# A second superblock's down projection as seven-product quads in one pipeline with gate and up

## The chip, the cores and the metric

The kernel runs on one core of a Trainium2 chip. The metric is the device time of one execution in microseconds. Three runs of the kernel before took 1899.77, 1903.79 and 1904.42 us; their median is 1903.79 us.

## The reference

One decoder layer over 2048 tokens of 1024 features, in float32:

```
xn = rmsnorm(x); z = xn @ w_in + b_in            # a, gate, p: 512 columns each
y_conv = silu(layernorm(causal_depthwise_conv31(a * sigmoid(gate))))
y_pool = per group of 128 channels: (trailing mean over 2/4/8/16 - token) @ w_pool, times a scale
h = x + concat(y_conv, y_pool) @ w_out
n = rmsnorm(h)
h = h + (silu(n @ w_gate) * (n @ w_up)) @ w_down  # 1024 -> 2816 -> 1024
out = rmsnorm(h)
```

## The kernel before, in words

The tokens are two superblocks (`a0`, `a1`, class `Sup`) of 1024 tokens, each two halves of 512. Features lie on the partitions, in tiles of 128. Each float32 operand of a product is split in two parts (`split`, L194): ScalarE casts the high part (L195), VectorE subtracts it for the low part (L196). A product is then three matmuls of 128x128 on 512 columns, high by high, high by low and low by high (`mm3`, L202 to L206). So each tile that goes into a product costs one ScalarE and one VectorE instruction.

SBUF is held in two arenas. `arena` has 17 slots for float32 staging, `arena_r` 36 units for split operands. Both give the range that has been free longest, in the order in which the program asks; activations (`R`) take four units, weights (`W`) two or one. PSUM has one `chain` tile of two banks and three tiles of two banks that `ps2` gives in turn.

The stages: input projection (`in_tile`, `in_evac`), convolution and pooling (mostly VectorE, woven in as a background generator), output projection and row norm (`mix_out`, `norm`), gate and up (`gate_up`), down (`down`, `down_last`), and the final norm.

Gate and up already use a seven-product scheme. A `Quad` is two output tiles by eight k-tiles by two halves, seen as a 2x2 by 2x2 block product, and done as seven products of 12 matmuls in place of eight. `put_t` forms the seven combinations of the activations (the factors `t[1]` to `t[7]`), `Quad.sums` and `Quad.put` the combinations of the weights, and `Quad.result` adds or multiplies what leaves PSUM. Bank copies on ScalarE (L911, L916, L918) keep partial sums between products, and the next product into that bank waits for them. In the steady loop of `gate_up` (L707 on) the products of a quad come in the order 1, 2, 6, 5, 7, 4, 3, with product 1 of the next quad ahead of 4 and 3. There are 22 quads, gate and up in turn, and each pair's product is stored in `at_d` (L926).

Down is done in three groups of four, four and three of these stored tiles (`GROUPS`). For each group `down_load` reads and splits the tiles, and `down` then runs eight output tiles, each with 8 k-tiles (6 in the last group) for both halves, adding to `h`, which it reads from and writes back to `h_d`. The weights are made by `Dense`, two ahead (`prime`). In the second superblock `down_last` does the last group together with the final norm.

`turn` joins the output projection and the first two quads: it steps generators by hand, so that the norm of the second half (`rows`: small matmuls for row sums, a power on POOL, a diagonal on VectorE; `spread`: matmuls that broadcast it; then scaling by L634) lies beside the first products. The order of the instructions on an engine follows the program, but the framework moves one ahead when by its own estimate an earlier one isn't ready; all DMAs of this part are issued on SP's queue in order.

Of the kernel before, what the change touches and what calls it, by code (L numbers as in the profile page):

```python
# [33 lines left out]
GROUPS = ((0, 4), (4, 8), (8, 11))  # L34
G32 = HALO + TT + 2
# [68 lines left out]
def block_kernel(ctx: ExitStack, tc: tile.TileContext, x, xt, wi, wo, wop, wg, wu, wd, wp, par, out):  # L104
# [44 lines left out]
    h_d = [dram(f"h_d{s}", NQ, 2 * TT) for s in range(NS)]  # L149
    at_d = [dram(f"at_d{s}", NFP, 2 * TT) for s in range(NS)]  # L150
# [34 lines left out]
    class W(Buf):  # L185


        WHERE = (range(8 * RU, NR), range(7 * RU, NR), range(NR))
# [19 lines left out]
    class Dense:  # L208


        def __init__(self, src, halves=False, parts=None):
# [22 lines left out]
        def mms(self, accs, ks, mov):  # L234

            ks = list(ks)
            for n, k in enumerate(ks):
                ww, c = self(k)
                r = mov[k // 2].v
                for b, acc in accs:  # L240
                    mm3(acc, ww, c, (r[:, 0, k % 2, b], r[:, 1, k % 2, b]), n == 0, n == len(ks) - 1)
# [26 lines left out]
    class Rms:  # L268
# [83 lines left out]
    class Sup:  # L352
# [176 lines left out]
        def ln(self):  # L529
# [21 lines left out]
            var.rows(1.0 / CC, LN_EPS, chain if first else None)  # L551
# [75 lines left out]
        def norm(self, b, hr):  # L627

            hr.rows(1.0 / D, RMS_EPS)
# [21 lines left out]
        def gate_up(self):  # L651
# [6 lines left out]
            at = None  # L658
            quads = []
            for n in range(2 * NFP):  # L660
                quads.append(Quad(self, n))
# [45 lines left out]
            for n in range(2, 2 * NFP):  # L707
# [25 lines left out]

        def down_load(self, g):
            a = []
# [7 lines left out]
            return a  # L743

        def down(self, g, a):
# [4 lines left out]
            ws = Ahead([lambda m=m: Dense(wd[g][m]) for m in range(KD)], 1)  # L750
            ws.prime(2)
# [19 lines left out]
        def down_last(self, g, a):  # L771

            n = len(a)
            ws = []
            ah = Ahead([lambda m=m: Dense(wd[g][m]) for m in range(KD)], 1)
# [55 lines left out]
    class Quad:  # L831
# [6 lines left out]
        at = None  # L838

        def __init__(self, sup, n):  # L840
# [5 lines left out]
            self.ch = chain_bank[n % 2]  # L846

# [27 lines left out]

        def result(self, a, b, acc, extra=None):
# [8 lines left out]

        def product(self, p):
            if p == 1:
                self.acc = ps2("quad")
                if self.gate:
                    Quad.at = B4("at")  # L890
                self.at = Quad.at
                self.o = self.at.v
            b1, b5, ch = self.acc[:, 0], self.acc[:, 1], self.ch
            dst = {1: b1, 2: b1, 5: b5, 3: b5}.get(p, ch)
            r = self.sup.t[p].v
# [9 lines left out]
            if self.n == 2 * NFP - 1:  # L905
                self.sup.t.pop(p).free()
# [15 lines left out]
            elif p == 3:  # L922
                self.result(0, 1, b5, self.s.v[:, 0])
                self.s.free()
                if not self.gate:
                    nc.sync.dma_start(at_d[self.sup.s][self.fp], self.at.ap)  # L926
                    self.at.free()
# [78 lines left out]
    pa1 = a0.in_tile(in0.get(), "pa")  # L1006
    a0.x_spread()
    a0.in_evac(0, pa, pg)
# [55 lines left out]
    def turn(s, gu):  # L1064
# [18 lines left out]
        nm = s.norm(1, s.hr)  # L1083
        step(gu)
        step(nm, 2)
        step(gu)
        step(nm)
# [10 lines left out]
    beside(a0.down(0, a0.down_load(0)), bg, 3, 1)  # L1098
    beside(a0.down(1, a0.down_load(1)), bg, 4, 1)
    run(bg)  # L1100
    dn = a0.down(2, a0.down_load(2))
# [70 lines left out]
```

## Time and profile before

| | |
|---|---|
| median of three runs | 1903.79 us |
| profiled execution | 1902.86 us |
| its span | 1901.1 us |
| TensorE matmul busy | 1841.0 us, 7995 records |
| VectorE busy | 1234.7 us |
| ScalarE busy | 623.2 us |
| HBM read, written | 189.19 MB, 73.49 MB |

The profiled execution is one run; its span goes from the first to the last instruction. A busy TensorE is no measure of its rate: matmuls overlap, so the start-to-start distance of matmuls and the number of records in a stretch say more. PEclk is the clock granted to TensorE, as a share of full speed. Some matmul records are missing.

### The profile page before, as it was taken

How to read it: one execution, taken by the hardware profiler on the slowest of the kernel's cores; microseconds unless marked ns; L12 is line 12 of the kernel's file. 1: busy time of each engine (PE TensorE's matmuls, PEld its weight loads, DVE VectorE, ACT ScalarE, POOL GpSimd, SP SyncE). 2: the span in 40 equal slices, each digit the busy share in tenths (PEclk: the TensorE clock that was granted, in tenths of full speed). 3: DMA queues.
4: the chain of work that ended last, by engine and by line, in shares of the span. 5: the costliest groups of instructions: out<-in, count | busy, mean ns of one | idle time of the engine just before them, and what ended most of it. 6: DMA issues, size and time to landing. Idle time of an engine off the chain costs nothing.

```text
span 1901.1 us, 19811 instructions
## 1 busy us (share of the span) xinstructions
PE 1841.0 (97%) x7995; PEld 1497.5 (79%) x7995; DVE 1234.7 (65%) x1359; ACT 623.2 (33%) x796; POOL 51.4 (3%) x41
## 2 busy tenths in 40 slices
PE   8999999998999999998999999899999999999996
PEld 6777887876788888877788888678888888888885
DVE  4989997488997999992542546866554545523235
ACT  5255124244333333341221323433333333412110
POOL 0103200000000000000000000000000000000000
PEclk9999999999999999998999999899999999999998
DMA  7263125523422232143583753155131113635422
GB/s 284 75 212 123 67 90 172 205 78 122 167 79 88 73 116 78 67 188 133 190 313 130 285 199 111 47 198 199 45 132 67 67 67 147 252 144 215 154 85 89
DMA packets 70235, 263.96 MB, mean 139 GB/s; under 512 B 7168, under 2 KB 11392, under 8 KB 56320
## 3 DMA queue, kind: packets, MB, share of 16 engines
q1 hardware_dynamic: 68848, 260.52, 38.1%
q10 hardware_dynamic: 1296, 2.19, 0.3%
q8 instruction: 62, 1.02, 0.2%
q14 instruction: 29, 0.24, 0.0%
HBM read 189.19 MB, written 73.49 MB: 138 GB/s over the span
## 4 chain that ended last, share of the span: by engine, by line
PE 83%; DVE 8%; DMA 4%; ACT 1%; issue 1%; POOL 0%; POOLq 0%; DVEq 0%; SPq 0%; ACTq 0%
PE pd L206 8%; PE pd L204 8%; PE pd L205 8%; PE quad L204 8%; PE quad L206 8%; PE quad L205 8%; PE chain L204 6%; PE chain L205 6%; PE chain L206 6%; PE px L204 3%; PE px L205 3%; PE px L206 3%; DVE arena_r L196 2%; DVE arena L491 2%; PE pa L206 1%
## 5 line engine op out<-in xcount | busy, mean ns | idle before, releaser
L195 ACT CAST arena_r<-arena 128x1024 fp32r<-128x1024 f32 (+3 forms) x375 | 364.4, 984 | 848.1 <-PE pd L205 228.9
L196 DVE TENSOR_TENSOR arena_r<-arena,arena_r 128x1024 fp32r<-128x1024 f32 (+3 forms) x375 | 422.2, 1138 | 246.5 <-ACT arena_r L195 215.5
L491 DVE SCALAR_TENSOR_TENSOR arena<-arena,par_sb 128x1024 f32<-128x1024 f32 (+1 forms) x240 | 287.2, 1212 | 2.3
L204 PE MATMUL quad<-arena_r 128*128 128x512 f32 x704 | 276.2, 393 | 11.7 <-ACT arena_r L195 10.8
L204 PE MATMUL pd<-arena_r 128*128 128x512 f32 x704 | 276.1, 392 | 9.9 <-ACT arena_r L195 9.1
L205 PE MATMUL quad<-arena_r 128*128 128x512 f32 x704 | 276.2, 392 | 0.8 <-DVE arena_r L196 0.8
L206 PE MATMUL pd<-arena_r 128*128 128x512 f32 x704 | 275.1, 391 | 1.8 <-DVE arena_r L196 1.8
L206 PE MATMUL quad<-arena_r 128*128 128x512 f32 x704 | 275.8, 392 | 0.0
L205 PE MATMUL pd<-arena_r 128*128 128x512 f32 x704 | 274.6, 390 | 0.0
L204 PE MATMUL chain<-arena_r 128*128 128x512 f32 x528 | 212.1, 402 | 4.9 <-ACT arena L916 2.8
L205 PE MATMUL chain<-arena_r 128*128 128x512 f32 x528 | 207.1, 392 | 0.9 <-DVE arena_r L196 0.9
L206 PE MATMUL chain<-arena_r 128*128 128x512 f32 x528 | 207.1, 392 | 0.0
L761 DVE TENSOR_TENSOR arena<-pd,arena 128x1024 f32<-128x1024 f32 x40 | 48.9, 1223 | 187.8 <-PE pd L206 186.7
L204 PEld LDWEIGHTS quad<-arena_r 128*128 128x128 f32 x704 | 133.3, 190 | 41.7 <-ACT arena_r L195 12.1
L204 PEld LDWEIGHTS pd<-arena_r 128*128 128x128 f32 x704 | 132.7, 188 | 39.1 <-ACT arena_r L195 10.2
L206 PEld LDWEIGHTS pd<-arena_r 128*128 128x128 f32 x704 | 132.5, 188 | 31.4 <-DVE arena_r L196 4.0
L205 PEld LDWEIGHTS quad<-arena_r 128*128 128x128 f32 x704 | 133.2, 189 | 29.3 <-DVE arena_r L196 1.9
L206 PEld LDWEIGHTS quad<-arena_r 128*128 128x128 f32 x704 | 133.3, 189 | 28.2 <-DVE arena_r L196 0.4
L205 PEld LDWEIGHTS pd<-arena_r 128*128 128x128 f32 x704 | 132.6, 188 | 27.9 <-issue 0.5
L204 PEld LDWEIGHTS chain<-arena_r 128*128 128x128 f32 x528 | 99.6, 189 | 38.0 <-ACT chain L911 8.8
L205 PEld LDWEIGHTS chain<-arena_r 128*128 128x128 f32 x528 | 99.9, 189 | 21.8 <-DVE arena_r L196 2.2
L206 PEld LDWEIGHTS chain<-arena_r 128*128 128x128 f32 x528 | 99.7, 189 | 21.8
(135 smaller groups left out, 2082.8 us busy)
## 6 DMA issues: line engine op xcount, KB each, us to landing
arena<-h_d SPq DMA_DIRECT2D x28, 1024.0 KB, 5.6
arena<-in_wg SPq DMA_DIRECT2D x44, 512.0 KB, 5.1
arena<-in_wu SPq DMA_DIRECT2D x44, 512.0 KB, 5.1
at_d<-arena SPq DMA_DIRECT2D x22, 1024.0 KB, 4.4
arena<-at_d SPq DMA_DIRECT2D x22, 1024.0 KB, 5.7
h_d<-arena SPq DMA_DIRECT2D x20, 1024.0 KB, 4.3
arena<-in_wd SPq DMA_DIRECT2D x32, 512.0 KB, 4.4
arena<-in_x SPq DMA_DIRECT2D x12, 1024.0 KB, 6.4
```

Of the source, the lines that this page charges most:

```text
L195: nc.scalar.copy(hi, y)
L196: tt(out=lo, in0=y, in1=hi.bitcast(F32), op=ALU.subtract)
L204: nc.tensor.matmul(acc, lhsT=w[:, 0, c], rhs=hi, start=start, stop=False, **kw)
L205: nc.tensor.matmul(acc, lhsT=w[:, 0, c], rhs=lo, start=False, stop=False, **kw)
L206: nc.tensor.matmul(acc, lhsT=w[:, 1, c], rhs=hi, start=False, stop=stop, **kw)
L491: stt(out=v, in0=u.ap[:, j : j + n], scalar=w, in1=v, op0=ALU.mult, op1=ALU.add)
L761: tt(out=v, in0=acc, in1=v, op=ALU.add)
```

## The change

For the second superblock the first two down groups become quads. `Quad.close` forms from each stored pair the seven combinations and writes them to a new scratch tensor `t_d` (four of them in place or untouched from the tile, three from a second tile `tx`, by four subtractions). `factors(g)` reads back and splits the seven factors of a group; it is stepped once per product of the last quad before the group, right where the old factor of that product number is freed (`follow`). `DownQuad` is a `Quad` with two tiles of `w_down` as weights, `h` as the tensor to add to, and the new factors. The eight down quads go into the same list as the 22, so the loop of `gate_up` runs over 30. `down_load` becomes a generator that is stepped in the same way in the last quad of either superblock and ends with the first two weight loads of the next `down`. The k-tiles of the down weights are laid out with the first halves of all tiles of a group ahead of the second halves (`pairs`, `place`).

Besides: the row norm of the second half uses a bank of the first quad, which is taken earlier (`begin`), and its rows stand after the first product in the order, its spread after the second. The spread of the first input norm stands ahead of the second input tile. Weights take units 28 to 35 in turn; before, 32 to 35 came first.

```diff
-        WHERE = (range(8 * RU, NR), range(7 * RU, NR), range(NR))
+        WHERE = (range(7 * RU, NR), range(NR))
...
-        def __init__(self, src, halves=False, parts=None):
+        def __init__(self, src, halves=False, parts=None, pairs=None):
+            self.place = (lambda k: (k % pairs, k // pairs)) if pairs else (lambda k: (k // 2, k % 2))
...
-            pv = ps2("pv") if bank is None else bank
-            f = flat(pv)
+            f = flat(ps2("pv")) if bank is None else bank
...
-            for n in range(2 * NFP):
-                quads.append(Quad(self, n))
+            quads = [Quad(self, n) for n in range(2 * NFP)]
+            if self.s:
+                self.td = [{} for _ in range(STRASSEN)]
+                for g in range(STRASSEN):
+                    quads[-1].follow = self.factors(g)
+                    quads += [DownQuad(self, g, q, len(quads) + q) for q in range(NQ)]
+                g = STRASSEN
+            else:
+                g = 0
+            quads[-1].follow = self.follow = self.down_load(g)
...
-            yield
-            for q in (q0, q1):
-                q.product(1)
-                q.product(2)
+            q0.begin()
+            q1.begin()
+            self.bank = q0.acc[:, 1]
+            yield
+            q0.product(1)
+            yield
+            q0.product(2)
+            yield
+            q1.product(1)
+            q1.product(2)
             q1.mid()
...
-            for n in range(2, 2 * NFP):
+            for n in range(2, len(quads) - 2):
...
+        def factors(self, g):
+            for p, i in ((1, 0), (2, 2), (6, 5), (5, 1), (7, 4), (4, 6), (3, 3)):
+                t = B4("tl")
+                nc.sync.dma_start(t.ap, t_d[g][:, i].rearrange("p n t -> p (n t)"))
+                self.td[g][p] = r = R("td")
+                for j in range(2):
+                    split(r.v[:, 0, j], r.v[:, 1, j], t.v[:, j])
+                t.free()
+                yield
...
         def down_load(self, g):
...
-            return a
+                yield
+            self.ws = Ahead([lambda m=m: Dense(wd[g][m], pairs=GROUPS[g][1] - GROUPS[g][0]) for m in range(KD)], 1)
+            self.ws.prime(2)
+            yield
...
+        def close(self):
+            if self.gate:
+                return
+            g, j = divmod(self.fp, 4)
+            if self.sup.s and g < STRASSEN:
+                o = self.o
+                tx = B4("tx")
+                for dst, i0, i1 in (
+                    (tx.v[:, 0, 0], o[:, 1, 1], o[:, 0, 1]),
+                    (o[:, 0, 1], o[:, 0, 1], o[:, 0, 0]),
+                    (tx.v[:, 0, 1], o[:, 1, 1], o[:, 0, 1]),
+                    (tx.v[:, 1, 0], o[:, 1, 0], tx.v[:, 0, 1]),
+                ):
+                    tt(out=dst, in0=i0, in1=i1, op=ALU.subtract)
+                nc.sync.dma_start(t_d[g][:, :4, j], self.at.ap.rearrange("p (n t) -> p n t", n=4))
+                nc.sync.dma_start(t_d[g][:, 4:, j], tx.ap[:, : 3 * T].rearrange("p (n t) -> p n t", n=3))
+                tx.free()
+            else:
+                nc.sync.dma_start(at_d[self.sup.s][self.fp], self.at.ap)
+            self.at.free()
...
-            if self.n == 2 * NFP - 1:
-                self.sup.t.pop(p).free()
+            if self.follow:
+                self.t.pop(p).free()
+                step(self.follow)
...
+    class DownQuad(Quad):
+        def __init__(self, sup, g, q, n):
+            self.sup, self.q = sup, q
+            self.s1, self.s2 = wd[g][2 * q], wd[g][2 * q + 1]
+            self.w = {}
+            self.ch = chain_bank[n % 2]
+            self.t = sup.td[g]
+            self.follow = None
+        def open(self):
+            self.h = B4("h")
+            nc.sync.dma_start(self.h.ap, h_d[self.sup.s][self.q])
+        def close(self):
+            nc.sync.dma_start(h_d[self.sup.s][self.q], self.h.ap)
+            self.h.free()
+        def result(self, a, b, acc, extra=None):
+            dst = self.h.v[:, a, b]
+            if extra is not None:
+                tt(out=dst, in0=dst, in1=extra, op=ALU.add)
+            tt(out=dst, in0=acc, in1=dst, op=ALU.add)
...
-    pa1 = a0.in_tile(in0.get(), "pa")
+    w = in0.get()
     a0.x_spread()
+    pa1 = a0.in_tile(w, "pa")
...
-        nm = s.norm(1, s.hr)
+        nm = s.norm(1, s.hr, s.bank)
         step(gu)
-        step(nm, 2)
+        step(nm)
         step(gu)
+        step(nm)
+        step(gu, 2)
         step(nm)
...
-    for g in range(len(GROUPS) - 1):
-        run(a1.down(g, a1.down_load(g)))
-    run(a1.down_last(len(GROUPS) - 1, a1.down_load(len(GROUPS) - 1)))
+    run(a1.follow)
+    for g in range(STRASSEN, len(GROUPS) - 1):
+        run(a1.down(g))
+        run(a1.down_load(g + 1))
+    run(a1.down_last(len(GROUPS) - 1))
```

## Rows read from the trace of the kernel before

**Rows 1.** The page, busy time of each engine, its share and instructions.
```profile
PE 1841.0 (97%) x7995; PEld 1497.5 (79%) x7995; DVE 1234.7 (65%) x1359; ACT 623.2 (33%) x796; POOL 51.4 (3%) x41
```

**Rows 2.** Timeline of PE, late gate/up of superblock 1: start, duration, engine, operation.
```profile
1611.77 0.39 PE L204 MATMUL quad<-arena_r 128*128 128x512 f32 x1
...
1612.45 0.39 PE L204 MATMUL quad<-arena_r 128*128 128x512 f32 x1
```

**Rows 3.** Windows: stretch, length, busy us (records) per engine, PEclk, DMA share, GB/s.
```profile
40.00:60.00 20.00, 16.84 (x68) 13.41 (x67) 10.45 (x9) 5.33 (x5) 0.38 (x2) 0.91 0.21 75
...
420.00:460.00 40.00, 31.54 (x122) 22.70 (x121) 33.65 (x38) 17.91 (x22) 1.01 (x1) 0.91 0.33 117
...
460.00:840.00 380.00, 379.11 (x1661) 309.91 (x1660) 350.96 (x382) 135.28 (x182) 0.00 (x0) 1.00 0.28 101
...
840.00:880.00 40.00, 30.56 (x124) 23.99 (x123) 16.30 (x17) 9.25 (x10) 0.00 (x0) 0.87 0.54 193
...
960.00:980.00 20.00, 20.00 (x89) 16.54 (x89) 2.96 (x4) 1.53 (x2) 0.00 (x0) 1.00 0.93 347
...
1200.00:1240.00 40.00, 31.97 (x113) 23.52 (x112) 33.06 (x39) 17.36 (x20) 1.01 (x1) 0.83 0.19 66
...
1240.00:1620.00 380.00, 380.00 (x1671) 310.44 (x1669) 202.16 (x252) 131.97 (x180) 2.48 (x1) 1.00 0.31 114
...
1620.00:1660.00 40.00, 39.51 (x173) 31.92 (x172) 26.33 (x26) 19.39 (x22) 0.00 (x0) 1.00 0.77 289
...
1660.00:1820.00 160.00, 160.00 (x708) 132.48 (x707) 46.18 (x40) 24.93 (x25) 0.00 (x0) 1.00 0.43 157
```

**Rows 4.** Groups by line, 1255 to 1620 us: busy us, mean ns, idle before.
```profile
L196 DVE TENSOR_TENSOR arena_r<-arena,arena_r 128x1024 fp32r<-128x1024 f32 x59 | 72.1, 1221 | 55.0 <-ACT arena_r L195 55.0
...
L195 ACT CAST arena_r<-arena 128x1024 fp32r<-128x1024 f32 x59 | 62.0, 1050 | 77.5 <-PE quad L205 75.2 <-DVE arena L866 2.3
```

**Rows 5.** DMA issues: count, KB each, median us from issue to landing.
```profile
arena<-at_d SPq DMA_DIRECT2D x22, 1024.0 KB, 5.7
```

**Rows 6.** Timeline of ScalarE at the superblock-1 seam, its idle time in brackets.
```profile
1640.52 4.84 ACT L195 CAST arena_r<-arena 128x1024 fp32r<-128x1024 f32 x5 [1.17 <-DMA arena<-at_d]
```

**Rows 7.** Timeline of all engines at the superblock-0 seam.
```profile
845.79 0.32 SPq L738 DMA_DIRECT2D arena<-at_d  x1
...
853.42 0.32 SPq L926 DMA_DIRECT2D at_d<-arena  x1
...
853.79 0.43 SPq L224 DMA_DIRECT2D arena<-in_wd  x1
...
859.57 1.04 ACT L195 CAST arena_r<-arena 128x1024 fp32r<-128x1024 f32 x1 [6.54 <-DMA arena<-in_wd]
...
860.67 0.80 PE L204 MATMUL pd<-arena_r 128*128 128x512 f32 x1 [8.73 <-ACT arena_r L195]
```

**Rows 8.** Timeline of the turn into superblock 1's gate/up.
```profile
1201.86 0.57 ACT L911 COPY chain<-quad 128x512 f32<-128x512 f32 x1 [0.94 <-PE quad L206]
...
1203.63 0.68 DVE L299 TENSOR_TENSOR arena<-arena 128x512 f32<-128x512 f32 x1
...
1207.16 0.95 PE L316 MATMUL pv<-ones,arena 128*128 128x1 f32 x8
...
1210.90 0.71 PE L346 MATMUL rb<-arena_r,ones_r 128*128 128x512 f32 x2
...
1211.78 2.06 DVE L634 SCALAR_TENSOR_TENSOR arena<-arena,par_sb,rb 128x512 f32<-128x512 f32 x3
...
1216.10 0.50 PE L204 MATMUL quad<-arena_r 128*128 128x512 f32 x1 [4.49 <-ACT arena_r L195]
```

**Rows 9.** Timeline of the start, around the second input tile.
```profile
48.35 0.40 PE L346 MATMUL chain<-arena_r,ones_r 128*128 128x512 f32 x1
...
50.55 1.22 DVE L411 TENSOR_TENSOR arena<-pg,arena 128x1024 f32<-128x1024 f32 x1
...
51.91 0.47 PE L204 MATMUL pg<-arena_r 128*128 128x512 f32 x1 [3.16 <-DVE arena L411]
```

More of the change, by code (lines that the diff above doesn't have):

```diff
@@ L34 @@
 GROUPS = ((0, 4), (4, 8), (8, 11))
+STRASSEN = 2
 G32 = HALO + TT + 2
@@ L149, in block_kernel @@
     h_d = [dram(f"h_d{s}", NQ, 2 * TT) for s in range(NS)]
+    t_d = [dr.tile([P, 7, 4, T], F32, name=f"t_d{g}", bufs=1) for g in range(STRASSEN)]
     at_d = [dram(f"at_d{s}", NFP, 2 * TT) for s in range(NS)]
@@ L238, in mms @@
                 ww, c = self(k)
[L239 removed]
+                i, h = self.place(k)
+                r = mov[i].v
                 for b, acc in accs:
[L241 removed]
+                    mm3(acc, ww, c, (r[:, 0, h, b], r[:, 1, h, b]), n == 0, n == len(ks) - 1)
         def free(self):
@@ L550, in ln @@
             yield
-            var.rows(1.0 / CC, LN_EPS, chain if first else None)
+            var.rows(1.0 / CC, LN_EPS, flat(chain) if first else None)
             yield
@@ L625, in mix_out, with norm @@
                     r.free()
-        def norm(self, b, hr):
-            hr.rows(1.0 / D, RMS_EPS)
+        def norm(self, b, hr, bank=None):
+            hr.rows(1.0 / D, RMS_EPS, bank)
             yield
@@ L742, in down_load, with down @@
                 t.free()
-            return a
-        def down(self, g, a):
+                yield
+            self.ws = Ahead([lambda m=m: Dense(wd[g][m], pairs=GROUPS[g][1] - GROUPS[g][0]) for m in range(KD)], 1)
+            self.ws.prime(2)
+            yield
+        def down(self, g):
+            a, ws = self.a, self.ws
             n = len(a)
@@ L749, in down @@
                 self.fr = Rms(whole=True)
-            ws = Ahead([lambda m=m: Dense(wd[g][m]) for m in range(KD)], 1)
-            ws.prime(2)
             for m in range(KD):
@@ L769, in down, with down_last @@
                 r.free()
-        def down_last(self, g, a):
+        def down_last(self, g):
+            a, ah = self.a, self.ws
             n = len(a)
             ws = []
-            ah = Ahead([lambda m=m: Dense(wd[g][m]) for m in range(KD)], 1)
             self.h = []
@@ L838, in block_kernel @@
         at = None
+        acc = None
         def __init__(self, sup, n):
@@ L874, in last @@
             self.st.free()
+        def open(self):
+            if self.gate:
+                Quad.at = B4("at")
+            self.at = Quad.at
+            self.o = self.at.v
+        def close(self):
+            if self.gate:
+                return
[16 more added lines that the diff above has]
+            self.at.free()
         def result(self, a, b, acc, extra=None):
@@ L884, in result, with begin @@
                 tt(out=dst, in0=acc, in1=dst, op=ALU.mult)
+        def begin(self):
+            if self.acc is None:
+                self.acc = ps2("quad")
         def product(self, p):
             if p == 1:
[L888 to L892, printed above, removed]
+                self.begin()
+                self.open()
             b1, b5, ch = self.acc[:, 0], self.acc[:, 1], self.ch
             dst = {1: b1, 2: b1, 5: b5, 3: b5}.get(p, ch)
-            r = self.sup.t[p].v
+            r = self.t[p].v
             key, u = self.USES[p]
@@ L924, in product, with open @@
                 self.s.free()
-                if not self.gate:
-                    nc.sync.dma_start(at_d[self.sup.s][self.fp], self.at.ap)
-                    self.at.free()
+                self.close()
+    class DownQuad(Quad):
[5 more added lines that the diff above has]
+            self.t = sup.td[g]
+            self.follow = None
+        def open(self):
+            self.h = B4("h")
[8 more added lines that the diff above has]
+            tt(out=dst, in0=acc, in1=dst, op=ALU.add)
     def fold():
@@ L1097, in block_kernel @@
     beside(g0, bg, 6, 6)
-    beside(a0.down(0, a0.down_load(0)), bg, 3, 1)
-    beside(a0.down(1, a0.down_load(1)), bg, 4, 1)
+    run(a0.follow)
+    beside(a0.down(0), bg, 3, 1)
+    run(a0.down_load(1))
+    beside(a0.down(1), bg, 4, 1)
     run(bg)
-    dn = a0.down(2, a0.down_load(2))
+    run(a0.down_load(2))
+    dn = a0.down(2)
     step(dn, 2)
```

8 lines of the change are left out of this document (4 added, 4 removed).

## The prediction

> **What bounds the kernel now.** I read the page's busy line first: TensorE is busy 1841 of 1901.1 us, no other engine over 65% [rows 1]. So time can only come from TensorE's work or from the 60 us in which it stands still, plus what it loses at the lower clock. The table of windows finds the second part. In an undisturbed stretch the matmuls are back to back: three of them start every 0.68 us [rows 2], 0.2267 us each, and the down stage keeps the same beat (708 records in 160 us; some records are missing) [rows 3]. Measured against that beat, four stretches fall short. At 40 to 60 us there are 68 matmuls where 88 fit: 20 x 0.2267 = 4.5 us lost. At 420 to 460 there are 122, worth 27.7 us: 12.3 lost. At 840 to 880 there are 124, worth 28.1: 11.9 lost. At 1200 to 1240 there are 113, worth 25.6: 14.4 lost. In all four the granted clock is below 1.00, so some of the loss is the stop and some is the half-rate restart [rows 3]. The seam between gate/up and down of the second superblock (1620 to 1660) has 173 of 176, a loss of under 1 us [rows 3]. A timeline of each short stretch then says what was late.
>
> **The change part by part.**
>
> *Fewer matmuls.* A down group of four tiles took 8 output tiles x 8 k-tiles x 2 halves x 3 = 384 matmuls. A seven-product form takes 4 quads x 7 products x 4 k-tiles x 3 = 336. Two groups save 96 matmuls: 96 x 0.2267 = 21.8 us [rows 2]. TensorE is back to back at 1.00 in that stage [rows 3], so all of it lies on the path. A quad is 84 x 0.2267 = 19.0 us, a product 2.72 us.
>
> *What it adds beside them.* Per down quad VectorE has three subtractions of 1.22 us and one of 0.68 for the weights' low parts, four of 0.68 for the weight sums and six of 0.68 for results: 11.1 us of 19.0; ScalarE has three casts of 1.05, one of 0.62 and three copies of 0.59, 5.5 us [rows 4, 8]; 0.62 and 0.59 are estimates for half the columns from the 1.05. That is covered. The four subtractions per up quad that form the factors are 2.7 us beside 202 us of VectorE in 380 [rows 3, 4], covered too. If that cover were gone they would cost 8 x 2.7 = 22 us.
>
> *The two changes of factor set.* This is the new risk. In the last up quad, and again in the last quad of the first group, seven factor tiles are loaded and split: 14 casts (14.7 us) and 14 subtractions (17.1 us) [rows 4]. Beside the quads' own 11.1 us each, VectorE has 17.1 + 22.2 = 39.3 us in the 38.1 us of two quads, so it runs late for a while. SyncE's transfers: seven loads of 1.05 MB, and per down quad 1.05 MB of weights and 2.1 MB of h: 7.3 + 6.3 = 13.6 MB in 38.1 us, or 357 GB/s, while the busiest window moved 347 [rows 3]. Against that: a factor tile can be written when the old factor of the same product number is done, and it is read about six products later, 16.3 us; load, cast and subtraction take 5.7 + 1.05 + 1.22 = 8.0 us [rows 4, 5]. So 8.3 us of slack each. Bounds for one changeover: 0, as the old seam shows under 1 us [rows 3], and 9.2 us, if VectorE's excess within a single quad (17.1 + 11.1 - 19.0) all lands on TensorE. I take 2.5 each, nearer the seam's row, since the splits spread over more than one quad: +5. Ends: 0 and +18.
>
> What stands in ScalarE's queue behind a late factor cast are the copies of a bank, for which the quad's next products wait; they have 2.72 us, one product. The old seam shows such a cast waiting 1.17 us for its load, with four more right behind it [rows 6]. The Trainium skill (TensorE: Matmul & The Clock Gate, Architectural detail: the array is 16× 32×32, not 1× 128×128) says that ScalarE and VectorE take their queues strictly in order, which speaks against this change; the trace agrees, in that nothing passed the cast. By that rule every load that is more than 2.72 us late is a stop of TensorE, which is the first rival below; by the row alone (1.17 us) it is covered.
>
> *The first superblock's seam.* Before, the store of the last up tile is issued at 853.42, when its result is there; only behind it in SP's queue come the first down weights at 853.79, their cast at 859.57, and the first matmul at 860.67, 8.73 us idle [rows 7]. Now the two first weight loads are issued in the fifth of the last quad's seven steps, ahead of that store. They still stand behind the last activation load (845.79) [rows 7]. Issued at about 846.2, landing 5.8 us later like the old one, and cast in 1.05: TensorE could start near 853.5, against 860.67, and keeps its clock. Of the 11.9 us lost I take 8 back. Ends: 0 (the load's staging slot is not free earlier) and -11.9. VectorE is at 351 of 380 us in the stage before [rows 3], because convolution work is woven in; the eight splits were already early in the old trace, so that load is not new. The down matmuls now take the k-tiles in the order first halves of all four tiles, then second halves, which asks for the fourth tile after 18 matmuls (4.1 us) and not 36; the fourth tile's load at 845.79 lands by about 851, so I cost this at nothing.
>
> *The two turns.* The sum for the row norm is complete at 1204.3 (1203.63 + 0.68); the row matmuls come at 1207.16, after three of four products, the spread 3.74 us later, VectorE's scaling at 1211.78, and TensorE stands 4.49 us until 1216.10 [rows 8]. Now the row matmuls come after the first product in the order, in a bank that a quad already has, and the spread after the second, so two products remain to cover the latency. The rows can then run at about 1204.5 to 1205: 2 to 2.7 us sooner, and VectorE's long chain behind them (33 of the 40 us busy [rows 3]) moves with it. What is late next is that chain itself, so the gain is its shift and some of the clock: I take 3 us a turn, 6 for both. Ends per turn: +2.4 (the first product is done when its bank is copied at 1201.86 [rows 8], and TensorE would stand until the sum at 1204.3) and -7 (half of what is lost there). Moved with it: one step of the quads is cut in three, no DMA issue moves.
>
> *The start.* The fourth spread matmul ran at 48.35, after the second input tile; so the first banks were drained at 50.55 and the next tile started at 51.91, after 3.16 us [rows 9]. With the spread ahead of the tile, the draining lies beside 48 matmuls. The window lost 4.5 us; I take 4. Ends: -4.5 and +1.6, if TensorE waits for the diagonal with nothing behind it; VectorE's convolution work then also starts sooner, which hides behind TensorE.
>
> *Weight slots and other loads.* Weights may use eight units in turn where four came first. No wait of TensorE in rows 3's full stretches depends on it: 0, ends -2 and +2.
>
> Sum: -21.8 + 5 - 8 - 6 - 4 = -34.8. The profiled execution took 1902.86 us (span 1901.1), 0.9 below the median of 1903.79. 1902.86 - 34.8 = 1868.
>
> **Rivals.**
>
> Late factors. Loads and splits of both changeovers land on TensorE, 9.2 us each and not 2.5. For it: the 357 GB/s and VectorE's 39.3 us. Against: 8.3 us of slack for each factor. 1868 + 13 = 1881.
>
> The order edits are hidden anyway. VectorE's chain in the turns, and the staging slot in the seam, set the same times as before, so only the matmuls go: 1902.86 - 21.8 + 5 = 1886. For it: VectorE's 33 of 40 us in the turns. Against: the store ahead of the weight loads is plain in SP's row.
>
> All edges close, and the clock stays up: -21.8 + 0 - 11.9 - 14 - 4.5 = -52, 1851 (1850.7). For it: the stops that drop the clock are all addressed. Against: VectorE still bounds the turns.
>
> Slower. The factor loads go one by one through SP's in-order queue, each holding until a staging slot is free, so that 14 factors come when they are needed and not 16.3 us sooner. Exposed in full that is 14 x 8.0 = 112 us; it makes the kernel slower as soon as each of them is on average over 2.8 us late past its slack (14 x 2.8 = 39.8, the sum without the 5). With half exposed, 4 us each, 1902.86 - 39.8 + 56 = 1919. For it: the old seam's cast that waits for its load. Against: the slack of 8.3 us is longer than one transfer of 5.7, so one load ahead is enough.
>
> That the change doesn't do what it says (a product count that comes out the same) can be left out: the loops give 336.
>
> **How the numbers follow.** Forecast 1868 (its own range 1858 to 1876): 0.50. Late factors, 1881: 0.20. Order edits hidden, 1886: 0.13. All edges, 1851: 0.12. Slower, 1919: 0.05. The range 1850 to 1885 takes in the forecast, most of the late factors, and about half of the two cases at its ends. Under 0.3% (5.7 us) is no change that can be told here. Faster by more than that: 0.93, where all but the last case lie; within it 0.03, the overlap of the hidden and slower cases; slower 0.04.
>
> **What would show it.** Right: 96 matmuls fewer, with a run of quads at 0.68 us per three from the last up quad to the last group; 840 to 880 with over 150 matmuls and a clock near 1.00; the wait of the next tile for the bank near 50 us gone; the spread in each turn 2 to 3 us after the end of the second product. Wrong: TensorE idle behind ScalarE's casts of factors at the two changeovers, or a longer wait at the row matmuls; a drop of the clock in the down quads would say that the late-factor case is the true one. The forecast falls if the time is above 1885 or below 1850.

## The result, and the profile after

The changed kernel takes 1873.72 us (median of four runs, 1872.33 to 1874.88), the kernel before 1904.11 (four runs on the same chip, 1899.77 to 1908.18). The ratio is 0.984 with an interval of 0.9817 to 0.9864: 30.4 us less, where the forecast said 34.8. The profiled execution took 1874.88 us, its span is 1873.1.

The busy line of the page of the changed kernel answers to [rows 1]: 96 matmul records fewer, and 79 us more of VectorE. No matmul record is missing on either side: before has 3696 of quads and 2112 of down products, just what the loops give.

```profile
PE 1822.0 (97%) x7899; PEld 1481.8 (79%) x7899; DVE 1313.8 (70%) x1483; ACT 661.8 (35%) x848; POOL 53.8 (3%) x41
```

The windows of the changed kernel answer to [rows 3], with the same columns. The stretches 40 to 60 and 840 to 880 are now full, at a clock of 1.00 (90 and 178 records, where before there were 68 and 124). The two turns are not: 420 to 460 has 122 records as before, 1200 to 1240 has 125. In the last three rows the down quads run at clock 1.00; 1660 to 1700 is full, the two rows of 60 us have 257 and 259 records where 264 fit.

```profile
40.00:60.00 20.00, 20.00 (x90) 16.57 (x89) 18.57 (x19) 3.78 (x4) 1.35 (x2) 1.00 0.24 79
420.00:460.00 40.00, 33.10 (x122) 23.99 (x121) 33.19 (x34) 18.13 (x22) 0.00 (x0) 0.91 0.30 105
840.00:880.00 40.00, 40.00 (x178) 32.99 (x177) 18.51 (x19) 9.46 (x11) 0.00 (x0) 1.00 0.60 212
...
1200.00:1240.00 40.00, 33.10 (x125) 23.90 (x124) 34.38 (x36) 18.41 (x23) 0.00 (x0) 0.91 0.29 105
1600.00:1660.00 60.00, 58.51 (x257) 47.59 (x257) 45.98 (x55) 32.77 (x40) 0.00 (x0) 1.00 0.70 259
1660.00:1700.00 40.00, 40.00 (x177) 32.83 (x176) 25.24 (x31) 15.96 (x19) 0.00 (x0) 1.00 0.61 222
1700.00:1760.00 60.00, 58.96 (x259) 47.99 (x258) 47.04 (x58) 25.50 (x32) 0.00 (x0) 1.00 0.70 261
```

Fixed windows move with the work, so I cut both traces at the same instructions instead: the last matmul of each mixing stage (`px`), the last matmul of the first superblock's last quad, its first layernorm matmul, and the row matmuls of the final norm. The table gives what each stretch gained or lost against the trace of before, in us; the last three columns are traces of experiments told below (turn_old, prime_back, no_quads).

| stretch | predicted | changed kernel | old turn order | weight loads back | quads off |
|---|---|---|---|---|---|
| start to last `px` of superblock 0 | -4 | -4.2 | -4.8 | -6.6 | -5.5 |
| turn 0, to the last quad's end | -3 | +3.1 | +2.0 | +0.6 | +2.8 |
| seam, to the first layernorm matmul | -8 | -12.2 | -12.2 | -0.4 | -12.2 |
| to the last `px` of superblock 1 | 0 | +1.6 | +0.1 | +1.6 | +0.1 |
| turn 1 and gate/up, to the row matmuls | -3 | +2.4 | -0.1 | +2.4 | +1.8 |
| down quads, to the last down matmul | -16.8 | -18.6 | -18.7 | -17.9 | -0.7 |

Turn 0 and the seam must be read together: in every trace with the early weight loads four down matmuls, 0.9 us, run ahead of the last quad's last product. Without these the changed kernel's turn 0 lost 2.2 and the seam gained 11.3.

### The profile page after: what moved, and what is told of

It reads as the page before. It is cut to its first block, busy times and chain, and to the rows that moved or that the text cites. A ratio compares the mean times of both kernels' runs of the same rounds, so it can differ in the third digit from the quotient of the medians.

```text
span 1873.1 us, 19893 instructions
## 1 busy us (share of the span) xinstructions
PE 1822.0 (97%) x7899; PEld 1481.8 (79%) x7899; DVE 1313.8 (70%) x1483; ACT 661.8 (35%) x848; POOL 53.8 (3%) x41
## 4 chain that ended last, share of the span: by engine, by line
PE 80%; DVE 11%; DMA 3%; issue 2%; ACT 1%; POOL 0%; SPq 0%; POOLq 0%; DVEq 0%; ACTq 0%
PE quad L206 10%; PE quad L207 9%; PE quad L208 9%; PE chain L206 8%; PE chain L207 7%; PE chain L208 7%; PE pd L206 5%; PE pd L208 5%; PE pd L207 5%; DVE arena_r L198 3%; DVE arena L494 3%; PE px L206 2%; PE px L207 2%; PE px L208 2%; DMA arena<-in_x 1%
## 5 line engine op out<-in xcount | busy, mean ns | idle before, releaser
L197 ACT CAST arena_r<-arena 128x1024 fp32r<-128x1024 f32 (+2 forms) x403 | 389.5, 980 | 773.5 <-PE quad L207 182.7
L198 DVE TENSOR_TENSOR arena_r<-arena,arena_r 128x1024 fp32r<-128x1024 f32 (+2 forms) x403 | 451.0, 1134 | 244.0 <-ACT arena_r L197 214.5
L206 PE MATMUL quad<-arena_r 128*128 128x512 f32 x832 | 326.5, 393 | 3.5 <-ACT chain L971 1.4
L207 PE MATMUL quad<-arena_r 128*128 128x512 f32 x832 | 325.6, 391 | 1.3 <-DVE arena_r L198 1.3
L208 PE MATMUL quad<-arena_r 128*128 128x512 f32 x832 | 325.2, 391 | 0.0
L206 PE MATMUL chain<-arena_r 128*128 128x512 f32 x624 | 250.5, 402 | 7.6 <-ACT arena L976 3.7
L207 PE MATMUL chain<-arena_r 128*128 128x512 f32 x624 | 245.5, 393 | 5.2 <-DVE arena_r L198 5.2
L208 PE MATMUL chain<-arena_r 128*128 128x512 f32 x624 | 245.1, 393 | 0.0
L206 PEld LDWEIGHTS quad<-arena_r 128*128 128x128 f32 x832 | 157.0, 189 | 39.5 <-ACT chain L971 2.3
L207 PEld LDWEIGHTS quad<-arena_r 128*128 128x128 f32 x832 | 157.3, 189 | 34.5 <-DVE arena_r L198 2.2
L208 PEld LDWEIGHTS quad<-arena_r 128*128 128x128 f32 x832 | 157.3, 189 | 32.9
L206 PE MATMUL pd<-arena_r 128*128 128x512 f32 x448 | 176.3, 393 | 1.3 <-DVE arena L820 0.8
L208 PE MATMUL pd<-arena_r 128*128 128x512 f32 x448 | 175.0, 391 | 1.1 <-DVE arena_r L198 1.1
L207 PE MATMUL pd<-arena_r 128*128 128x512 f32 x448 | 175.0, 391 | 0.0
L206 PEld LDWEIGHTS chain<-arena_r 128*128 128x128 f32 x624 | 118.1, 189 | 47.2 <-ACT chain L971 14.1
L207 PEld LDWEIGHTS chain<-arena_r 128*128 128x128 f32 x624 | 118.5, 190 | 29.6 <-DVE arena_r L198 6.7
L208 PEld LDWEIGHTS chain<-arena_r 128*128 128x128 f32 x624 | 118.3, 190 | 25.2
L206 PEld LDWEIGHTS pd<-arena_r 128*128 128x128 f32 x448 | 84.4, 188 | 20.1 <-DVE arena L820 1.2
L206 PE MATMUL px<-arena_r 128*128 128x512 f32 x256 | 100.2, 392 | 0.1
L208 PEld LDWEIGHTS pd<-arena_r 128*128 128x128 f32 x448 | 84.5, 189 | 19.4 <-DVE arena_r L198 1.6
L207 PE MATMUL px<-arena_r 128*128 128x512 f32 x256 | 99.7, 389 | 0.0
```

Source lines behind the costliest of these rows:

```text
L197: nc.scalar.copy(hi, y)
L198: tt(out=lo, in0=y, in1=hi.bitcast(F32), op=ALU.subtract)
L206: nc.tensor.matmul(acc, lhsT=w[:, 0, c], rhs=hi, start=start, stop=False, **kw)
L207: nc.tensor.matmul(acc, lhsT=w[:, 0, c], rhs=lo, start=False, stop=False, **kw)
L208: nc.tensor.matmul(acc, lhsT=w[:, 1, c], rhs=hi, start=False, stop=stop, **kw)
```

## The experiments

Each is the changed kernel with one edit. Medians are each beside runs of the kernel before on the same chip, and so are the ratios.

**The turns in their old order (turn_old, bank_only).** The first undoes order and bank, the second only the order.

```diff
-            q0.begin()
-            q1.begin()
-            self.bank = q0.acc[:, 1]
             yield
-            q0.product(1)
-            yield
-            q0.product(2)
-            yield
-            q1.product(1)
-            q1.product(2)
+            for q in (q0, q1):
+                q.product(1)
+                q.product(2)
...
-        nm = s.norm(1, s.hr, s.bank)
+        nm = s.norm(1, s.hr)
         step(gu)
-        step(nm)
+        step(nm, 2)
         step(gu)
         step(nm)
         step(gu, 2)
         step(nm)
-        step(gu, 2)
-        step(nm)
```

bank_only keeps the three lines with `begin` and `self.bank` and the `s.bank` argument, and has the rest.

> The changed kernel with the turn as before: rows of the second half's norm after the four products, spread right behind, in a PSUM tile of their own. Theory: the row matmuls, moved up, stand on TensorE for the sum (2.18 us), the clock falls behind that stop, and both turns cost 3.1 + 2.35 us more than before. Then the time is 1873.7 - 5.4 = 1868.3 us. Rival: the turns got slower because of the new weight slots or of the earlier start, not of the order: then it stays at 1873 to 1875.

> The changed kernel with the old order of rows and spread in the turns, but with the row sums in the first quad's bank as in the change. Theory: the order alone costs, so this is as fast as the kernel with the whole old turn, 5 to 6 us (0.3%) below the changed kernel, with no 2 us stop ahead of the row matmuls. Rival: the bank, which is taken earlier, costs: then it is as slow as the changed kernel.

Measured: turn_old 1870.06, ratio 0.98 (0.9787 to 0.9813); bank_only 1868.83, ratio 0.9813 (0.9798 to 0.9828). Neither lost what a useful turn edit would have given; turn 1 cost -0.1 and -0.2 in them against +2.4. The bank is not what matters.

**The rows one product later (rows_late).** A `yield` between the third and the fourth product; the row matmuls stand behind the second in the program, the spread behind the third. In the order as built the rows come after 35 of the four products' 48 matmuls:

```diff
             q1.product(1)
+            yield
             q1.product(2)
...
-        step(gu)
+        step(gu, 2)
         step(nm)
```

> The changed kernel with the row matmuls behind the first quad's second product, and the spread behind the second quad's first. In the order as built, the rows stand behind 31 of the 48 matmuls and the spread 5 matmuls further. Theory: the sum is there by then, so the 2.2 us stop ahead of the rows goes, but the spread now stands for the diagonal, 3.7 us behind the rows, of which 5 matmuls cover 1.1: a stop of 2.6 us in its place, and a time like the changed kernel's, 1870 to 1875 us. Rival: only the stop at the rows counts: then it is as fast as with the old turn, 1868 us.

Measured: 1871.21, ratio 0.9827 (0.9812 to 0.9841); turn 1 cost +0.7. TensorE no longer waits for the sum, and the stop of 2.6 us that I expected at the spread was 0.2; but behind it the next products wait 3.0 us for their first cast. I had that place wrong.

**The first down weights back behind the store (prime_back).**

```diff
-            self.ws.prime(2)
+            if self.s:
+                self.ws.prime(2)
...
+            if not self.s:
+                ws.prime(2)
```

> The changed kernel, but in the first superblock the first two down weights are asked for when the group begins, as before; the activations are still read in the last quad. Theory: the weight load behind the store of the last up tile is the whole seam, so its 12.2 us come back: 1886 us, and TensorE stands about 8.7 us ahead of the first down matmul. Rival: the earlier reading of the activations made the gain; then under 3 us come back: below 1877 us.

Measured: 1883.96, ratio 0.9868 (0.9855 to 0.9882). The seam's whole gain is gone, -12.2 to -0.4. Over the whole run less came back than the 12 us that I expected: the ratios differ from the changed kernel's (0.984, and 0.9829 in after_again) by 5 to 7 us. In this trace the start gained 2.4 us more, and turn 0 lost 1.6 less, than in the changed kernel's, and the edit touches neither.

**The start: the spread back (spread_back), the weight slots back (where_back).**

```diff
-    w = in0.get()
+    pa1 = a0.in_tile(in0.get(), "pa")
     a0.x_spread()
-    pa1 = a0.in_tile(w, "pa")
```

```diff
-        WHERE = (range(7 * RU, NR), range(NR))
+        WHERE = (range(8 * RU, NR), range(7 * RU, NR), range(NR))
```

> The changed kernel with the first norm's spread behind the second input tile, as before. Theory: TensorE is 5 to 7 us later by 108 us, but 2.8 of it are given back in the pooling tiles, where it waits for a weight load, so the end is 4.4 us later: 1878 us. Rival: the start is all given back later: 1874 us. Other rival: nothing is given back: 1881 us.

> The changed kernel with weights in units 32 to 35 first, as before. Theory: no wait of TensorE hangs on it, so within 2 us of the changed kernel. Rival: the rotation over eight units is what lets casts run ahead in the down quads: then 3 to 6 us slower, with new stops at the changeovers.

Measured: 1875.99, ratio 0.9828 (0.9815 to 0.9841), and 1876.44, ratio 0.9851 (0.9835 to 0.9868). By the ratios spread_back is no slower than the changed kernel (0.984 and 0.9829), where 4.4 us were expected. where_back, expected within 2 us, is 4.3 us above after_again on the same chip, with intervals that just overlap; its new stops lie at the start and not at the changeovers.

**The quads off (no_quads), in one group only (one_group).** `STRASSEN = 2` becomes 0 and 1.

> The changed kernel with no down group as quads: the second superblock's three groups as before, 96 matmuls more, all other edits kept. Theory: the quads are worth 21.8 us of matmuls less 3 us of stops at the two changeovers: 1873.7 + 18.6 = 1892.3 us. Rival: the matmuls count in full and the stops are elsewhere: 1895.5 us. Rival: the quads' gain is partly given back at the last group: below 1888 us.

> The changed kernel with only the first down group as quads, the other two as before. Theory: each group is worth half, 10.9 us of matmuls less its own changeover, so half of the 18.5 us from the first superblock's final row matmuls on: 1873 + 9.2 = 1882 us. Rival: the second changeover costs what the first doesn't: then the first alone gives over 11 us, 1880 us or less.

Measured: 1888.09, ratio 0.9894 (0.988 to 0.9907), and 1882.55, ratio 0.9877 (0.9861 to 0.9894). From the row matmuls of the first superblock's final norm to the last down matmul no_quads gains 0.7 us, one_group 9.7, two groups 18.6: so 9.0 for the first group and 8.9 for the second. As a whole no_quads lost 10 to 12 us by the ratios, less than the 18.6 expected; the stretch itself lost 17.9, and the rest of the difference lies in stretches that the edit doesn't touch and that differ from one execution to the next (after_again shows by how much).

**What the changeovers wait for (no_sums, loads_twice, pool_sums).** no_sums leaves out the four weight sums of each down quad, so its quads multiply by other weights; loads_twice issues each factor's load twice; pool_sums puts the sums on GpSimd.

```diff
+        def sums(self):
+            self.put("d", self.m[:, 1:2], 1)
```

```diff
                 nc.sync.dma_start(t.ap, t_d[g][:, i].rearrange("p n t -> p (n t)"))
+                nc.sync.dma_start(t.ap, t_d[g][:, i].rearrange("p n t -> p (n t)"))
```

```diff
+            self.put("d", m[:, 1:2], 1)
+            pt = nc.gpsimd.tensor_tensor
+            pt(out=m[:, 1], in0=m[:, 0], in1=m[:, 1], op=ALU.add)
...
+            pt(out=m[:, 3], in0=m[:, 3], in1=m[:, 2], op=ALU.subtract)
```

> The changed kernel; left out are the four weight sums of each down quad, whose products then use the raw weights. Theory: at the changeovers VectorE is late, the sums come behind the factors' low parts, and casts and bank copies stand behind the sums; without them the stops of 1.49, 0.71 and 0.33 us go, and the stretch from the final norm's row matmuls of the first superblock to the end of the second's is 3 us shorter: 1869 to 1871 us. Rival: the factors' loads are late: the stops stay, and the time too.

> The changed kernel with each of the 14 factor loads done twice, one behind the other. Theory: the loads have 8.3 us of slack over their 5.7 us, so a second load costs at most 2 us in all. Rival of the prediction (late factors): the transfers are at the limit at the changeovers, so 14.7 MB more cost 5 us or more at each, 10 us and over.

> The changed kernel with the four weight sums of each down quad on POOL and not on VectorE. Theory: at the changeovers a cast stands for a weight sum that is late on VectorE behind the factors' low parts, and a bank copy stands behind that cast, so TensorE loses 3 us in all (1.49, 0.71 and 0.33 us and the restarts); with the sums on POOL these stops go: 2 to 3 us faster. Rival: the loads of the factors are late: then the stops stay. Rival: POOL is slower than the slack of 10.9 us allows for four sums, or slows VectorE: then it gets slower.

Measured: no_sums 1871.35, ratio 0.9825 (0.981 to 0.9839); loads_twice 1875.84, ratio 0.9854 (0.9837 to 0.9871); pool_sums 1880.55, ratio 0.9876 (0.9861 to 0.989). Between the same two marks they gained 19.4, 15.9 and 8.6 us against 18.6. So no_sums gained 0.8 in place of the 3 us expected, loads_twice lost 2.7 where at most 2 were expected, and pool_sums got slower where 2 to 3 us of gain were expected.

**The changed kernel again (after_again).**

> The changed kernel unaltered, on the chip of the runs beside it, to compare them with: 0.984 of the kernel before, and a trace within 2 us of the first one at each mark.

Measured: 1872.15, ratio 0.9829 (0.9813 to 0.9845). The trace did not stay within 2 us: it is 2.3 us ahead of the first at the end of turn 0 and 3.9 at the last `px` of superblock 1. So a single trace gives the turns and the start to 2 or 3 us only; the seam (-12.2) and the down quads (-18.4) repeat within 0.2.

## Why the prediction was right, and where its terms were off

The total came within 6 us of the forecast and inside its own range. The terms did not all come as they were argued: two were too small, one had the wrong sign, and one was made in part by an edit that I had costed at nothing. In part the total is luck: the turns came out 10.6 us worse than written, and the seam and the quads, 3.3 and 1.8 better, made up half of that. (One product in the prediction is off without effect: 14 x 2.8 is 39.2; for 39.8 each factor must be 2.84 us late.)

**Fewer matmuls: right, and the changeovers smaller than feared.** The stretch gains 18.6 of the 21.8 us (17.9 against no_quads, which has the other edits), so the changes of factor set cost 3 to 4 us, not 5. Three stops add up to that: measured from matmul start to matmul start, less the beat of 0.23, they are 1.65 us at 1631, 0.48 at 1708 and 0.87 at 1729, together 3.0. (A fourth, of 0.85 us, stands earlier, at 1265, where a quad waits for VectorE; it is there in the traces with the new turn order and quads, and not with the old order. Before had 1.2 us of stops of its own between the two marks, so about half a microsecond stays unaccounted for.) The four extra subtractions per up quad cost next to nothing: 1240 to 1600 has 1580 records at clock 1.00, of 1588 that fit. The list of TensorE's waits in the changed kernel from 1600 to 1800 (waiting line, what it waited for, total, times, longest) names them:

```profile
PE chain L206 <- ACT chain L971: 2.2, 2, 1.5
PE quad L206 <- DVE arena L1010: 0.3, 1, 0.3
```

The stop is a bank copy (L971) that came late. What held it is seen in the timelines of VectorE and of ScalarE at the first changeover, in the changed kernel:

```profile
1620.54 6.89 DVE L198 TENSOR_TENSOR arena_r<-arena,arena_r 128x1024 fp32r<-128x1024 f32 x6
1627.35 0.68 DVE L896 TENSOR_TENSOR arena<-arena 128x512 f32<-128x512 f32 x1
1627.95 1.22 DVE L198 TENSOR_TENSOR arena_r<-arena,arena_r 128x1024 fp32r<-128x1024 f32 x1
1629.09 0.68 DVE L897 TENSOR_TENSOR arena<-arena 128x512 f32<-128x512 f32 x1
```

```profile
1629.81 1.04 ACT L197 CAST arena_r<-arena 128x1024 fp32r<-128x1024 f32 x1 [1.06 <-DVE arena L897]
1630.76 0.58 ACT L971 COPY chain<-quad 128x512 f32<-128x512 f32 x1
```

```profile
1629.51 0.39 PE L208 MATMUL quad<-arena_r 128*128 128x512 f32 x1
1631.39 0.50 PE L206 MATMUL chain<-arena_r 128*128 128x512 f32 x1 [1.49 <-ACT chain L971]
```

VectorE works without a gap: six splits in a row and then the weight sums L896 and L897. The cast of a weight sum waits 1.06 us for L897, the copy stands behind the cast, and TensorE, whose product ended at 1629.51, waits 1.49 for the copy. The prediction had this chain (a cast ahead of a bank copy) but with another cause: it feared the factors' loads. In ScalarE's list of waits from 1595 to 1780 no cast waits for a load; the longest wait for another engine than TensorE is the sum's:

```profile
ACT arena_r L197 <- PE quad L207: 29.8, 19, 3.8
...
ACT arena_r L197 <- DVE arena L897: 9.7, 3, 5.0
```

no_sums tells how much of it the sums are. Its list of the same stretch:

```profile
PE chain L206 <- ACT chain L971: 0.7, 1, 0.7
PE quad L206 <- DVE arena L1013: 0.5, 1, 0.5
```

The stop of 1.5 is gone, the stops fall from 3.0 to 1.6 us (0.87 and 0.68, measured as above), the stretch gains 0.8. So the sums caused the longest stop, and what makes the other 1.6 stays open. Doubling every factor load, 14 more transfers of 1 MB, costs 2.7 us in the stretch: the loads have some room there, but not for twice their number. The slower rival, loads late by 4 us each, was far off, and so was the late-factor rival's 9.2 a changeover: no cast waits for a load, so the 8.3 us of slack held. The Trainium skill (TensorE: Matmul & The Clock Gate, Architectural detail: the array is 16× 32×32, not 1× 128×128) says that ScalarE and VectorE serve their queues strictly in order; the trace agrees, with the copy that starts as the 1.04 us cast ends.

GpSimd can't relieve VectorE here. The groups by line of GpSimd in pool_sums (busy, mean ns, idle before):

```profile
L1003 POOL TENSOR_TENSOR arena<-arena 128x512 f32<-128x512 f32 x8 | 16.0, 2001 | 0.6
L1005 POOL TENSOR_TENSOR arena<-arena 128x512 f32<-128x512 f32 x8 | 13.4, 1672 | 0.6
L1004 POOL TENSOR_TENSOR arena<-arena 128x512 f32<-128x512 f32 x8 | 12.0, 1504 | 12.8 <-DVE arena_r L198 12.6
...
L1002 POOL TENSOR_TENSOR arena<-arena 128x512 f32<-128x512 f32 x8 | 11.0, 1378 | 450.3 <-DVE arena_r L198 450.3
```

Four sums take 6.6 us one after the other, against 4 x 0.68 = 2.7 on VectorE. TensorE then waits 7.6 us in four places from 1600 to 1800, each for a VectorE result:

```profile
PE quad L206 <- DVE arena L1019: 7.6, 4, 3.5
```

That VectorE's own in-order work stands behind the splits of these late sums is the likely reason; the runs show the slow sums and the waits, not the link.

**The first superblock's seam: right mechanism, 8 us taken and 11.3 there.** SyncE's timeline of the changed kernel, where `at_d` are the stored activations, `in_wd` are down weights and L931 is the store:

```profile
817.37 13.31 SPq L764 DMA_DIRECT2D arena<-at_d  x3
835.81 0.32 SPq L784 DMA_DIRECT2D arena<-h_d  x1
837.27 0.33 SPq L227 DMA_DIRECT2D arena<-in_wd  x1
842.41 3.73 SPq L784 DMA_DIRECT2D arena<-h_d  x3
852.31 0.32 SPq L931 DMA_DIRECT2D at_d<-arena  x1
852.68 0.43 SPq L227 DMA_DIRECT2D arena<-in_wd  x1
```

I had put the first weights behind the last activation load, and that load at 845.79, where the old trace has it. In the changed kernel the last activation load goes out by 830.7, and the first weight load at 837.27, 15 us ahead of the store. Only this one of the two passed the store; the second still stands behind it, at 852.68, and holds nothing up. So nothing of the stop was left, and its clock loss went with it: TensorE goes from the last quad into the down products in one beat.

```profile
850.44 0.39 PE L208 MATMUL quad<-arena_r 128*128 128x512 f32 x1
850.67 0.39 PE L207 MATMUL pd<-arena_r 128*128 128x512 f32 x1
```

The counter-test is prime_back. Its SyncE timeline, and TensorE's:

```profile
847.36 0.32 SPq L934 DMA_DIRECT2D at_d<-arena  x1
847.73 0.42 SPq L227 DMA_DIRECT2D arena<-in_wd  x1
```

```profile
845.50 0.39 PE L208 MATMUL quad<-arena_r 128*128 128x512 f32 x1
854.59 0.80 PE L206 MATMUL pd<-arena_r 128*128 128x512 f32 x1 [8.71 <-ACT arena_r L197]
```

With the loads behind the store the stop is 8.71 us, where before it was 8.73 [rows 7], and the seam's gain is 0.4. The activations are read early there too, so it is not their earlier load that made the gain. That is the clearest of the shown causes: the place of one weight load in SyncE's queue, about 11 us. The all-edges rival was right about this edge.

**The turns: wrong sign.** The step that failed is that the rows run "2 to 2.7 us sooner, and VectorE's long chain behind them (33 of the 40 us busy [rows 3]) moves with it", at 3 us a turn. The end of its range that the prediction named, that TensorE would stand until the sum, is what happened. The changed kernel's timeline of the second turn:

```profile
1187.89 0.39 PE L208 MATMUL px<-arena_r 128*128 128x512 f32 x1
...
1191.52 0.69 DVE L303 TENSOR_TENSOR arena<-arena 128x512 f32<-128x512 f32 x1 [0.70 <-ACT arena L289]
...
1192.27 1.87 PE L319 MATMUL quad<-ones,arena 128*128 128x1 f32 x8 [2.18 <-DVE arena L303]
...
1194.98 0.63 PE L207 MATMUL quad<-arena_r 128*128 128x512 f32 x1
...
1195.41 0.63 PE L208 MATMUL quad<-arena_r 128*128 128x512 f32 x1
...
1195.81 1.29 DVE L337 TENSOR_TENSOR arena_r<-ident,rs 128x512 fp32r<-128x512 f32 x2
...
1199.37 0.63 PE L349 MATMUL rb<-arena_r,ones_r 128*128 128x512 f32 x2
...
1200.04 1.41 DVE L637 SCALAR_TENSOR_TENSOR arena<-arena,par_sb,rb 128x512 f32<-128x512 f32 x2 [2.95 <-PE rb L349]
```

The row matmuls did run sooner after the last `px` matmul: 4.38 us (1192.27 - 1187.89) against 7.54 before (1207.16 [rows 8] - 1199.62, its start in that trace). But TensorE stood 2.18 us for the sum; then the product between the rows and the spread runs at the low clock, a matmul every 0.43 us and not 0.23. So the spread, in order behind it, comes 7.10 us after the rows, against 3.74 [rows 8], and VectorE starts to scale 12.15 us after the last `px`, against 12.16 before. In this execution the chain did not move at all, and the stop was added.

Does the shift pay where the clock stays up behind the rows? In where_back the same order had the same stop (2.24 us), and no drop right behind it. Windows of 6 us behind the rows, the changed kernel first, then where_back:

```profile
1193.00:1199.00 6.00, 5.75 (x17) 4.69 (x17) 1.70 (x5) 0.00 (x0) 1.01 (x1) 0.50 0.07 27
```

```profile
1196.00:1202.00 6.00, 5.75 (x26) 4.66 (x26) 3.71 (x8) 2.48 (x3) 1.01 (x1) 1.00 0.04 14
```

There VectorE's scaling starts 9.30 us after the last `px`, 2.9 sooner than before, more than the shift that I counted on, and at the 74th product matmul behind that `px` TensorE is 2.2 us ahead of before. But the clock falls later in the same turn, and turn 1 costs +0.8 in the end:

```profile
1219.00:1228.00 9.00, 7.81 (x18) 5.64 (x19) 6.86 (x6) 4.65 (x6) 0.00 (x0) 0.50 0.18 73
```

So order and clock must be told apart. These are the 45 us behind the last `px` in the changed kernel, where_back, pool_sums (whose edit doesn't touch the turns) and bank_only:

```profile
1187.89:1232.89 45.00, 35.67 (x125) 25.91 (x124) 36.67 (x42) 18.51 (x22) 1.01 (x1) 0.85 0.18 62
```

```profile
1190.68:1235.68 45.00, 35.63 (x131) 25.44 (x129) 37.31 (x42) 19.02 (x23) 1.01 (x1) 0.89 0.19 63
```

```profile
1187.32:1232.32 45.00, 35.70 (x138) 25.98 (x137) 37.92 (x44) 19.10 (x23) 1.01 (x1) 0.92 0.25 90
```

```profile
1185.19:1230.19 45.00, 35.61 (x135) 26.54 (x134) 36.94 (x42) 19.08 (x23) 1.01 (x1) 0.89 0.23 79
```

With a clock of 1.00 or 0.50 these means stand for about 13.5, 10, 7 and 10 us at the lower level. Ten of the traces have the new order, all with the stop for the sum, and their turn 1 costs +1.8 to +2.4 where 13.5 us are low (six traces), +0.5 to +0.8 where 10 are (three), and -0.7 in pool_sums. The old order, with 10 us low, costs -0.1 and -0.2. In turn 0, read at the 168th product matmul, the new order costs +1.6 with 7 us low (after_again, prime_back) and +3.9 to +5.1 with 13.5 (six traces), the old order +3.0 and +3.2 with 13.5. (Before, the zero of these costs, had 7 us low in turn 0 and 13.5 in turn 1.) At equal time at the low clock the new order is the dearer one by 0.6 to 2 us a turn; the rest of what it lost in the changed kernel is clock, and that differs from one execution to the next.

In the old order TensorE stops once, and later, for the scaled operand. bank_only's wait from 1180 to 1245:

```profile
PE quad L206 <- ACT arena_r L197: 4.4, 1, 4.4
```

rows_late, between the two orders, splits it: no stop for the sum, 3.0 at that cast, +0.7. The products that may run before the scaled operand is there are the same four in every order; the new order waits for that operand under 1 us (0.3 for its cast, 0.6 for its low part), but puts a stop of 2.2 us among them. By the cuts of the table the old order costs 1.8 to 1.9 us over both turns, the new one 2.6 (after_again) to 5.6 (5.5 in the changed kernel); as a whole, 0.98 and 0.9813 against 0.9829 and 0.984, the intervals overlap. The best version that was run is thus the change without its turn order, at 1869 to 1870 us; that it is faster than the change itself the medians suggest but do not settle. The rival "order edits are hidden anyway" was nearer for the turns, where nothing was gained, and wrong for the seam.

**The start: the size right, the reasons half.** The wait of the second tile for the bank, 3.16 us [rows 9], is gone in the changed kernel, and comes back in spread_back. The wait lists from 36 to 60 of spread_back, and from 60 to 110 of where_back; the changed kernel's lists of both stretches are empty:

```profile
PE pg L206 <- DVE arena L414: 2.5, 1, 2.5
```

```profile
PE fold L206 <- ACT arena_r L197: 1.9, 2, 1.0
```

The second row is the error: I costed the weight slots at nothing (-2 to +2), and without them TensorE stops twice at the folding products, as it did before (1.7 us). At the first pooling tile the changed kernel is 7.2 us ahead of before, spread_back 4.0 and where_back 3.6; so spread and slots gave about 3 us each there, not 4 and 0. Of the 7.2 the next 300 us give 3 back, most of it in one wait for a weight's cast, in the changed kernel's list from 100 to 165:

```profile
PE pp L206 <- ACT arena_r L197: 3.3, 1, 3.3
```

So net 4.2 came where 4 was written, out of two gains and one loss that were not in the sum. The 4.2 is one draw besides: in the eleven traces with the same start it is 3.5 to 6.6, in spread_back 2.2 and in where_back 2.1.

**What stays open.** Why the same stop of 2.2 us is followed by the low clock in some executions of the new order (in turn 1 the changed kernel and after_again among them) and not in others (where_back, spread_back, pool_sums); the 1.6 us of the changeovers that no_sums leaves; and the 1.6 us between the seam and the second turn in some traces: in the changed kernel the granted clock is 0.94 and 0.89 in the two 10 us from 900 to 920, in after_again 1.00.

## What to carry to other kernels

Look first for loads that stand behind a store in an in-order queue at a change of stage: a weight load that went out ahead of one store, and not behind it, gave about 11 us, more than half of what 96 fewer matmuls gave. Before moving a latency chain's first step earlier, check what the engine would wait for there: a stop moved to an earlier place is still a stop, and at a place where no product can be run meanwhile it gained nothing here. Where a stage gets denser, sum each engine's work over the busiest quad, not over the stage: VectorE is 73% busy from 1600 to 1780 (131 of 180 us), and still its six splits in a row, with the weight sums behind them, made TensorE's longest stop there.

## What the runs showed of the hardware that was not expected

GpSimd takes 1.38 to 2.00 us for a 128x512 float32 sum or difference (pool_sums), where VectorE takes 0.68: two to three times as long. The Trainium skill (GPSIMD Engine Reference, 3.1 Elementwise — side-by-side cycle accounting) gives 1.96 for an add of 2048 columns; the one add of the four, L1002 at 1378 ns for 512, is 2.0 times VectorE's and fits it. Of the three subtractions L1003, at 2001 ns, is 2.9 times and does not. And a stop of TensorE has no fixed price: 2.18 us in the changed kernel and 2.24 in where_back, at the same instruction, were followed by a granted clock of 0.50 in one and 1.00 in the other. Over ten executions of that turn in the same order the time at the low clock went from about 7 to 13.5 us, and the turn's cost from -0.7 to +2.4.
